# A build-time schedule with other durations for products and transfers (hybrid decoder, fp32 by split products)

## The chip, the cores and the metric

The kernel runs on one core of one Trainium2 chip. The time is the device time of one execution in microseconds; a version's time is the median of its runs. The engines are TensorE (PE, with its weight loads as PEld), VectorE (DVE), ScalarE (ACT), GpSimd (POOL) and the DMA queues (SP's, ACT's and POOL's among them). Each engine carries out its own instructions in the order in which they were emitted.

## The reference

Two layers of a decoder trunk, computed for a prompt of 2048 tokens and for 8 samples of one token each, all float32, width 1024. Cut to the parts that matter here:

```python
# layer 0: one projection feeds a convolution module and a gated delta rule
p = rms_norm(x, g) @ w_in
glu_val, glu_gate, gate_a, qkv, z, beta_l, a_l = split(p)
c = depthwise_conv31(glu_val * sigmoid(glu_gate))
a_out = silu(layer_norm(c + dw_b)) * silu(gate_a)
q, k, v = silu(depthwise_conv4(qkv))
b_out = rms_norm(gated_delta_rule(l2norm(q), l2norm(k), v, beta, g)) * silu(z)
x = x + concat(a_out, b_out) @ w_out
# layer 1: windows of 2, 4, 8, 16 tokens on four channel groups
u, gate = split(rms_norm(x, g) @ w_in_odd)
x = x + ((group_linear(window_mean(u) - u)) * scale * silu(gate)) @ w_out_odd
# behind each of the two: attention to a memory of 256 rows
x = x + softmax(rms_norm(x, g) @ wq @ mem_k.T / 16) @ mem_v @ wo
y = rms_norm(x, g)
```

The prompt and the samples share the weights. The samples have their own convolution states, delta-rule states and memory caches. The new states and the projected memory (keys and values) are outputs too.

## The kernel before

**Products.** A float32 operand is split into a high part (rounded to fp32r) and the rest. Each product is then three fp32r products: high by high, low by high, high by low. The splits of a weight tile `rraw` are the tiles `rhi` (a cast, on ScalarE or VectorE) and `rlo` (a subtraction, on VectorE or GpSimd); those of an activation are `hh`/`hl`, `h`, `xh`/`xl`, `mh`/`ml` by stage. `ps_mm` names the PSUM tile of all these products; there are three banks of it. The small float32 products of the side work go to the pool `bgp` (`ps_bg`, `ps_ss`, `ps_bc`, `ps_cs` and others).

**Stages.** There is one stream of 15,920 `ps_mm` products, the dense stream. It runs through the memory's keys and values (products of 256 columns), phase 1 (the input projection, `dense_main`, in pieces of 512, 512, 512, 512 and 260 tokens), the fill (`Fill.run`: memory keys times query weights and values times output weights, into DRAM tensors `d_G` and `d_VW` by way of `gv`), `e2` (layer 0's output projection, first product `xh,rhi`), the attention of layer 0, the odd mixer and the attention of layer 1.

**Side work.** Everything else hangs on that stream as generators:

- `conv31` runs 8 halves of the 31-tap convolution on VectorE, each of 30 steps `cacc<-glu,dww,cacc` of 1024 columns, 240 in all; `conv4` runs the 4-tap one (`qacc`).
- `fin_val` writes `glu`, which also frees a PSUM bank of the dense stream.
- `sample_mix` is the samples' mixer of layer 0; its first TensorE product is `ps_cs<-m_sq,ones`.
- `phase2` is the delta rule, in chunks, beside the fill.
- `sample_attn` is the samples' attention; it reads the caches into `a_big` and has row sums spread through DRAM tensors `d_sq` and `d_sp`.
- `square_sum`, `token_rstd` (`ps_ss`) and `spread` (`ps_bc`) are the norm's three steps: sum of squares, reciprocal root per token, and its spreading over the partitions.

**What sets the order.** The class `Flow` (L56 to L387) emits every instruction, and it keeps an assumed time for each engine in `t`. An instruction starts, by this account, when its engine is free and its operands are there, and takes a cost that is a formula in the number of columns. For VectorE and ScalarE these are, for instance, columns/0.96 + 130 ns for `scalar_tensor_tensor` with a scalar operand (L222) and columns/1.2 + 51 or more for an activation (L175). After each dense product, `pump` (L342) looks through the side tasks. It takes the next step of the first one whose own assumed time is not beyond that of TensorE, as long as neither ScalarE nor VectorE is ahead of TensorE by more than a limit (L62: 1500 or 3500 ns). So assumed costs alone fix where in the dense stream each side instruction stands, on every engine. They also choose engines: `move` and `rows` choose between ScalarE and VectorE, and `ve` between GpSimd and VectorE, by which would be done first by the assumed times. A store that has only ScalarE behind its data goes to ScalarE's DMA queue, any other to SP's (L294). A DMA's assumed landing decides when the tasks that read it may go on.

The costs that the change touches are in `mm` (L163) and `_dma` (L292); `spread` (L437) and `tok_spread` (L1486) are touched too.

Of the kernel before, what the change touches and what calls it, by code (L numbers as in the profile page):

```python
# [7 lines left out]
F32 = mybir.dt.float32  # L8
F32R = mybir.dt.float32r
# [14 lines left out]
def fsz(ap):  # L24
    n = 1
    for s in ap.shape[1:]:
        n *= s
    return n
# [27 lines left out]
class Flow:  # L56
# [106 lines left out]
    def mm(self, out, lhsT, rhs, start=True, stop=True, cost=None):  # L163
        n = fsz(rhs)
        if cost is None:
            cost = max(n, 248) * 0.422 if lhsT.dtype == F32R else max(n, 64) * 1.69
        self.pe_op(cost, out, lhsT, rhs)
        self.nc.tensor.matmul(out, lhsT, rhs, start=start, stop=stop)  # L168

# [122 lines left out]
    def _dma(self, out, in_, eng, t):  # L292
        ri, ro = [self.region(in_)], [self.region(out)]
        if eng == "sync" and out.space == DRAM and self.hand.get(in_.tensor.name) == {"act"}:  # L294
            eng = "scalar"
        s = max(self.t[eng], t, self.ready(ri, ro, eng))
        nb = 4
        for _, c in out.ap:
            nb *= c
        if eng == "scalar":  # L300
            s = max(s, self.t["act"])
            self.t["act"] = self.t[eng] = g = s + 360
        elif eng == "gpsimd":
            s = max(s, self.t["pool"])
            self.t["pool"] = self.t[eng] = g = s + 1060
        else:
            self.t[eng] = s + 50
            s = max(s, self.hw)
            self.hw = g = s + 475
        x = max(g + 650, self.ring)  # L310
        self.ring = x + nb / 360.0
        self.mark(ri, ro, "dma", self.ring, self.ring + 900)
        getattr(self.nc, eng).dma_start(out=out, in_=in_)

    def split(self, hi, lo, src, eng="dve", scale=1.0):
# [121 lines left out]
def spread(F, C, pool, ppool, r, n, tag, dg=None):  # L437

    ncn = (n + 127) // 128
    if dg is None:  # L440
        dg = pool.tile([128, ncn * 128], F32, tag=tag + "dg", name="dg")
    for c in range(ncn):
        F.ts(dg[:, c * 128:(c + 1) * 128], C.ident, r[:, c:c + 1], ALU.mult)
    yield
    ps = ppool.tile([128, 512], F32, tag="bg", name="ps_bc")
    F.mm(ps[:, 0:n], C.ones, dg[:, 0:n])
    return ps


def ceil128(n):  # L450
    return (n + 127) // 128 * 128
# [200 lines left out]
def phase1(F, C, I, D, st, P, R, mmp, bgp, loaders, mix, hp):  # L652
# [38 lines left out]
    with F.tile_pool(name="x1", bufs=1, side="right") as xp:  # L691
# [59 lines left out]
        def norms():  # L751
            for t, (o, n) in enumerate(DT):
                yield lambda: t in sums and (t < 4 or "kv" in sums)
                dg = xp.tile([128, 512], F32, tag="dg", name="dg", bufs=1)
                bc = yield from spread(F, C, xp, bgp, sums[t], n, "n", dg)
                for k in range(8):
                    x, _ = xs.pop((t, k))
                    F.stt(x, x, C.g_mix[:, 0, k:k + 1], bc[:, 0:n], ALU.mult, ALU.mult)
                    if k == 7:
                        F.now()  # L760
                    yield
                    F.copy(hs(t, 0, k), x)
                    yield
                    F.tt(hs(t, 1, k), x, hs(t, 0, k).bitcast(F32), ALU.subtract, eng=F.ve(n))
                    hfree.give()
                yield
                hdone.add(t)
# [716 lines left out]


def tok_spread(F, C, W, r, n):  # L1486
    return spread(F, C, W.p, W.bgp, r, n, "w", dg=W.t("sqq", [128, ceil128(n)]))


def mm3(F, R, W, name, j, x, n):  # L1490
# [12 lines left out]
def e2(F, C, W, I, D, st, R, bdone, over, grow, spawn):  # L1503
# [7 lines left out]
    def norm():  # L1511

        for g in range(NG):
            n = gn(g)
            yield lambda: g < 2 or g - 2 in used
            c = W.t("cd"[g % 2], [128, 4, n])
            load_cols(F, c, cv, g)
            yield
            cs = W.t("sqa", [128, n])
            F.red(cs, kt(c), ALU.add)  # L1520
            yield
            ps = W.bgp.tile([128, 512], F32, tag="bg", name="ps_mean")
            F.mm(ps[:, 0:n], C.ones, cs)
            F.stt(c, ps[:, 0:n].unsqueeze(1).to_broadcast([128, 4, n]), -1.0 / 512, c, ALU.mult, ALU.add)
            yield
            acc = square_sum(F, W, c, n)
            yield
            r = tok_rstd(F, C, W, acc, n, 1.0 / 512)
            yield
            ps = yield from tok_spread(F, C, W, r, n)  # L1530
            F.tt(c, c, ps[:, 0:n].unsqueeze(1).to_broadcast([128, 4, n]), ALU.mult)
            yield
            for q in range(4):
                F.act(c[:, q, :], c[:, q, :], AF.Silu, scale=C.lng[:, q:q + 1], bias=C.lnb[:, q:q + 1])
            ln[g] = c
# [71 lines left out]
def attn(F, C, W, D, st, R, l, xin, xout):  # L1607
# [130 lines left out]
    def final(g, y):  # L1738
        yield W.sq.ok
        W.sq.take()  # L1740
        acc = None
        for h in range(2):
            acc = square_sum(F, W, y[h], 256, acc, h == 1, "pool" if g < NG - 1 else "dve")
        yield
        r = tok_rstd(F, C, W, acc, 256, 1.0 / 1024)
        yield
        ps = yield from tok_spread(F, C, W, r, 256)
        W.sq.give()
        for j in range(8):
            h, q = j // 4, j % 4  # L1750
            F.stt(y[h][:, q, :], y[h][:, q, :], C.g_fin[:, j:j + 1], ps[:, 0:256], ALU.mult, ALU.mult)
            if q % 2:
                F.dma(D.o_y[g][:, j - 1:j + 1], y[h][:, q - 1:q + 1, :])
        if g + 2 < NG:
            ys[g + 1] = load_y(g + 1)
        ydone.add(g)
# [23 lines left out]
def odd_u(F, C, W, I, D, st, R, rr):  # L1780
# [5 lines left out]
    def prep():  # L1786
        for g in range(NG):
            n = gn(g)
            yield lambda: ("x", "o", g) in st.done and (g > 0 or "s0" in st.done)
            res = W.xbuf if g % 2 == 0 else W.mbuf  # L1790
            acc = None
            for h in range(2):
                x = W.t("f", [128, 4, n])
                F.dma(x, D.x2[g][:, 4 * h:4 * h + 4])
                yield
                acc = square_sum(F, W, x, n, acc, h == 1)
                if h == 0:
                    yield res.ok
                    res.take()
                    xs = W.pair("x" if g % 2 == 0 else "m", n)  # L1800
                yield from split_steps(F, xs[0][:, 4 * h:4 * h + 4], xs[1][:, 4 * h:4 * h + 4], x)
            ready[g] = xs, res
            yield
            r = tok_rstd(F, C, W, acc, n, 1.0 / 1024)
            F.vcopy(rr[:, g, 0:r.shape[1]], r)
            yield
            ps = yield from tok_spread(F, C, W, r, n)
            if g == 0:
                W.rb = W.t("rb", [128, 2, 264])
            rdone[g] = W.rb[:, g % 2, 0:n]  # L1810
            F.vcopy(rdone[g], ps[:, 0:n])
# [831 lines left out]
```

## Time and profile before

| | |
|---|---|
| median of 3 runs | 2902.09 us (2898.34 to 2905.38) |
| profiled execution | 2902.86 us, span 2901.1 us |
| mean granted TensorE clock in it | 0.972 |
| busy: TensorE, VectorE, ScalarE, GpSimd | 94%, 68%, 36%, 23% of the span |
| mean DMA rate | 130 GB/s |

By the dense stream's place, the trace has the memory products up to some 95 us, phase 1 from there to 826 us, the fill with the delta rule from 826 to 1164 us, and `e2` from 1200 us on. The odd mixer and the two attentions take the rest. The shares are means over stages that differ: VectorE's 68% is 94% in part of phase 1 and 54% at the end of it. A row of a group of instructions gives line, engine, operation, tile written and tiles read, shape and count, then the busy time and the mean duration in ns, then the idle time of the engine just ahead of them with what ended it. A row of the timeline gives start and duration in us, and in brackets the idle time before it. A float32 product leaves two records in the trace, an fp32r product one.

### The profile page before, as it was taken

To read this page: it belongs to the slowest core of one execution; us is meant where nothing else is said; L and a number is where in the kernel's file an instruction comes from. 1 tells how busy PE (TensorE), PEld (TensorE's weight loads), DVE (VectorE), ACT (ScalarE), POOL (GpSimd) and SP (SyncE) were. 2 spreads that over 40 slices of the span, in tenths; PEclk is the share of its full clock that TensorE was granted. 3 is DMA by queue.
4 is the path that set the end of the run, shared out by engine and by line. 5 is a ranking of instruction groups with operands and counts; after the bars stand their busy time and mean duration, and the time that the engine had idled before them with its cause. 6 is when DMAs were issued, how large, how long until landed. Compare 5 with 4: busy or idle time off the path is not lost.

```text
span 2901.1 us, 52440 instructions
## 1 busy us (share of the span) xinstructions
PE 2730.5 (94%) x20202; PEld 2498.5 (86%) x20202; DVE 1968.4 (68%) x4612; ACT 1032.0 (36%) x2448; POOL 657.0 (23%) x936
## 2 busy tenths in 40 slices
PE   7999999999998889799999999899999998999997
PEld 6878888888888778699898889899999997789987
DVE  6838999988667887776655556867755445765453
ACT  5632232233356455432321325443422122432321
POOL 3301112111054355122232320111011111221210
PEclk9999999999989899899999999999999999999998
DMA  7611122123455557565645434322545556422211
GB/s 240 213 48 41 46 75 65 46 77 113 129 148 160 154 165 230 172 228 183 211 149 169 144 117 140 116 70 74 173 134 165 181 165 206 136 78 68 70 59 52
DMA packets 269194, 377.85 MB, mean 130 GB/s; under 512 B 46096, under 2 KB 168208, under 8 KB 268944
## 3 DMA queue, kind: packets, MB, share of 16 engines
q1 hardware_dynamic: 211776, 264.77, 29.4%
q0 software_dynamic: 20864, 67.39, 7.5%
q10 hardware_dynamic: 36304, 42.34, 4.2%
q8 instruction: 159, 2.61, 0.4%
q14 instruction: 91, 0.75, 0.1%
HBM read 276.38 MB, written 96.40 MB: 128 GB/s over the span
## 4 chain that ended last, share of the span: by engine, by line
PE 34%; DMA 9%; DVE 6%; issue 2%; ACT 1%; POOL 1%; DVEq 0%; SPq 0%; POOLq 0%; ACTq 0%
PE ps_mm L168 32%; DMA a_big<-d_sp 2%; DVE a_big L225 1%; DMA a_big<-d_sq 1%; DMA a_big<-in_cache_v 1%; PE ps_pt L172 1%; DMA w_f<-d_x 1%; DVE rlo L225 1%; DVE w_d L219 1%; DMA rraw<-d_VW 1%; PE ps_row L168 1%; DVE rlo L219 1%; DVE ml L219 0%; DMA rraw<-d_G 0%; DMA a_big<-in_cache_k 0%
## 5 line engine op out<-in xcount | busy, mean ns | idle before, releaser
L219 POOL TENSOR_TENSOR rlo<-rraw,rhi 128x512 fp32r<-128x512 f32 x143 | 209.1, 1470 | 579.0 <-ACT rhi L186 495.5
L225 DVE SCALAR_TENSOR_TENSOR cacc<-glu,dww,cacc 128x1024 f32<-128x1024 f32 x240 | 325.6, 1369 | 5.9 <-ACT cacc L186 1.4
L219 POOL TENSOR_TENSOR w_sqb<-w_sqb,w_sqq 128x512 f32<-128x512 f32 (+1 forms) x101 | 137.1, 1357 | 660.9 <-ACT w_sqq L186 653.9
L168 PE MATMUL ps_mm<-xh,rhi 128*128 128x256 f32 (+1 forms) x1920 | 274.0, 285 | 5.3 <-DVE pool_sm L219 3.2
L168 PE MATMUL ps_mm<-xl,rhi 128*128 128x256 f32 (+1 forms) x1920 | 273.1, 284 | 0.0
L168 PE MATMUL ps_mm<-xh,rlo 128*128 128x256 f32 (+1 forms) x1920 | 272.7, 283 | 0.0
L168 PEld LDWEIGHTS ps_mm<-xh,rhi 128*128 128x128 f32 x1920 | 250.6, 192 | 8.6 <-issue 3.4
L168 PEld LDWEIGHTS ps_mm<-xl,rhi 128*128 128x128 f32 x1920 | 250.0, 192 | 2.6
L168 PEld LDWEIGHTS ps_mm<-xh,rlo 128*128 128x128 f32 x1920 | 248.2, 191 | 1.0
L168 PE MATMUL ps_mm<-hh,rhi 128*128 128x512 f32 (+2 forms) x1152 | 216.8, 329 | 20.2 <-ACT hh L186 15.8
L219 DVE TENSOR_TENSOR w_y<-ps_mm,w_y 128x256 f32<-128x256 f32 (+1 forms) x248 | 103.4, 420 | 165.6 <-PE ps_mm L168 161.2
L168 PE MATMUL ps_mm<-hh,rlo 128*128 128x512 f32 (+2 forms) x1152 | 214.6, 328 | 0.0
L168 PEld LDWEIGHTS ps_mm<-hh,rhi 128*128 128x128 f32 x1152 | 177.9, 191 | 42.0 <-ACT hh L186 16.2
L168 PE MATMUL ps_mm<-hl,rhi 128*128 128x512 f32 (+2 forms) x1152 | 211.7, 326 | 0.0
L225 DVE SCALAR_TENSOR_TENSOR a_big<-a_big 128x256 f32<-128x256 f32 x256 | 105.0, 448 | 144.5 <-DMA a_big<-d_sp 78.3
L186 ACT ACTIVATE rhi<-rraw 128x512 fp32r<-128x512 f32 x235 | 143.8, 628 | 164.0 <-DMA rraw<-d_G 41.5
L168 PEld LDWEIGHTS ps_mm<-hh,rlo 128*128 128x128 f32 x1152 | 175.9, 191 | 19.4 <-issue 2.2
L168 PEld LDWEIGHTS ps_mm<-hl,rhi 128*128 128x128 f32 x1152 | 175.4, 190 | 17.3
L168 PE MATMUL ps_mm<-mh,rhi 128*128 128x256 f32 (+1 forms) x1152 | 170.1, 288 | 11.8 <-ACT mh L186 11.7
L168 PE MATMUL ps_mm<-ml,rhi 128*128 128x256 f32 (+1 forms) x1152 | 170.5, 290 | 2.5 <-DVE ml L219 2.5
L168 PEld LDWEIGHTS ps_mm<-mh,rhi 128*128 128x128 f32 x1152 | 153.6, 195 | 14.5 <-ACT mh L186 12.8
L168 PE MATMUL ps_mm<-mh,rlo 128*128 128x256 f32 (+1 forms) x1152 | 165.6, 284 | 0.0
(425 smaller groups left out, 5344.5 us busy)
## 6 DMA issues: line engine op xcount, KB each, us to landing
w_f<-d_x SPq DMA_DIRECT2D x60, 512.0 KB
d_x<-w_y SPq DMA_DIRECT2D x44, 512.0 KB
w_y<-d_x SPq DMA_DIRECT2D x44, 512.0 KB
a_big<-in_cache_k POOLq DMA_DIRECT2D x64, 256.0 KB, 4.0
a_big<-in_cache_v POOLq DMA_DIRECT2D x64, 256.0 KB, 4.1
rraw<-in_w_in SPq DMA_DIRECT2D x56, 256.0 KB
d_qkv<-so ACTq DMA_DIRECT2D x48, 256.0 KB
rraw<-in_w_xk SPq DMA_DIRECT2D x32, 256.0 KB
```

Source lines behind the costliest of these rows:

```text
L168: self.nc.tensor.matmul(out, lhsT, rhs, start=start, stop=stop)
L172: self.nc.tensor.transpose(out, in_, ident)
L186: self.nc.scalar.activation(out=out, in_=in_, func=func, scale=scale, **kw)
L219: self._e(eng).tensor_tensor(out=out, in0=a, in1=b, op=op)
L225: self._e(eng).scalar_tensor_tensor(out=out, in0=a, scalar=s, in1=b, op0=op0, op1=op1, **kw)
```

## The change

It alters two assumed costs and the moment at which one pool is looked up.

```diff
@@ class Flow, mm
         if cost is None:
-            cost = max(n, 248) * 0.422 if lhsT.dtype == F32R else max(n, 64) * 1.69
+            cost = max(n, 240) * 0.426 + 9 if lhsT.dtype == F32R else max(n, 64) * 1.69
@@ class Flow, _dma
-        x = max(g + 650, self.ring)
-        self.ring = x + nb / 360.0
-        self.mark(ri, ro, "dma", self.ring, self.ring + 900)
+        x = max(g + 925, self.ring)
+        self.ring = x + nb / 270.0
+        self.mark(ri, ro, "dma", self.ring, self.ring + 1000)
@@ spread
     yield
-    ps = ppool.tile([128, 512], F32, tag="bg", name="ps_bc")
+    ps = getattr(ppool, "bgp", ppool).tile([128, 512], F32, tag="bg", name="ps_bc")
@@ tok_spread
-    return spread(F, C, W.p, W.bgp, r, n, "w", dg=W.t("sqq", [128, ceil128(n)]))
+    return spread(F, C, W.p, W, r, n, "w", dg=W.t("sqq", [128, ceil128(n)]))
```

An fp32r product of 512 columns is now assumed to take 227.1 ns instead of 216.1, one of 260 119.8 instead of 109.7, and one of 256 118.1 instead of 108.0. A transfer of 256 KB is assumed to start 925 instead of 650 ns behind its issue, to occupy the ring for 971 instead of 728 ns, and to be seen 1000 instead of 900 ns later. The costs of VectorE, ScalarE and GpSimd stay as they were. `spread` is a generator that stops at `yield`, and the pool of `ps_bc` is now asked for when it goes on, not when it is called.

The dense stream keeps its order, and each engine has the same kinds of work; the side instructions stand elsewhere in the stream. Some also change their engine: 25 casts `rhi` and 8 copies `gv` go from ScalarE to VectorE, 2 `rlo` from GpSimd to VectorE, and a few rows of the delta rule from VectorE to ScalarE.

The first place is on TensorE in phase 1, around the first product of the samples' mixer, `ps_cs<-m_sq,ones` (`h` and `hh`/`hl` are the split activations, `rhi`/`rlo` the split weights). Before:

```order
L168 MATMUL ps_mm<-h_223,rhi 128x512
L168 MATMUL ps_mm<-h_224,rhi 128x512
L168 MATMUL ps_mm<-h_225,rhi 128x512
L168 MATMUL ps_cs<-m_sq,ones 128x64
L168 MATMUL ps_mm<-h_210,rlo 128x512
L168 MATMUL ps_mm<-h_211,rlo 128x512
```

Now:

```order
L168 MATMUL ps_mm<-hh_244,rhi 128x512 x8
L168 MATMUL ps_mm<-hl_245,rhi 128x512 x8
L168 MATMUL ps_mm<-hh_244,rlo 128x512 x8
L168 MATMUL ps_mm<-hh_239,rhi 128x512 x8
L168 MATMUL ps_mm<-hl_240,rhi 128x512 x8
L168 MATMUL ps_mm<-hh_239,rlo 128x512 x8
L168 MATMUL ps_cs<-m_sq,ones 128x64
L168 MATMUL ps_mm<-hh_234,rhi 128x260 x8
L168 MATMUL ps_mm<-hl_235,rhi 128x260 x8
```

`ps_cs` stands 64 dense products earlier: 48 of 260 columns and 16 of 512 that were ahead of it are now behind it.

The second place is on VectorE, the rows ahead of `m_sq`, which `ps_cs` reads (the `m_` tiles are the mixer's). Before:

```order
L225 SCALAR_TENSOR_TENSOR cacc<-glu,dww,cacc 128x1024 x2
L232 TENSOR_SCALAR m_s<-m_s 128x96
L242 RECIPROCAL m_s<-m_s 128x96
L225 SCALAR_TENSOR_TENSOR cacc<-glu,dww,cacc 128x1024 x2
L219 TENSOR_TENSOR m_s<-m_s,m_x 128x96
L219 TENSOR_TENSOR m_sq<-m_s 128x64
L219 TENSOR_TENSOR rlo<-rraw,rhi 128x512
L225 SCALAR_TENSOR_TENSOR cacc<-glu,dww,cacc 128x1024 x2
L232 TENSOR_SCALAR m_sq<-ps_cs 128x64
```

Now:

```order
L225 SCALAR_TENSOR_TENSOR cacc<-glu,dww,cacc 128x1024 x2
L232 TENSOR_SCALAR m_s<-m_s 128x96
L242 RECIPROCAL m_s<-m_s 128x96
L225 SCALAR_TENSOR_TENSOR cacc<-glu,dww,cacc 128x1024 x2
L219 TENSOR_TENSOR m_s<-m_s,m_x 128x96
L219 TENSOR_TENSOR m_sq<-m_s 128x64
L232 TENSOR_SCALAR m_sq<-ps_cs 128x64
L415 TENSOR_SCALAR ri<-m_sq 128x64
```

Around it the rows are nearly the same, but ahead of `m_sq` there are now 238 of the 240 `cacc` steps instead of 224, and no work stands between `m_sq` and the reading of `ps_cs`.

The third place is on TensorE at the end of the fill (`rhi`, `rlo` with no `x` are the fill's operands; `x`, `vn`, `qk`, `o` are the delta rule's, `w_sqa` the next stage's norm). Before, the last rows of 95 side products in a row:

```order
L168 MATMUL ps_bg<-x,A 128x128 x4
L168 MATMUL ps_mean<-w_sqa,ones 128x256
L168 MATMUL ps_bg<-vn,kd 128x128 x4
L168 MATMUL ps_bg<-vn,qk 128x128 x4
L172 MATMUL ps_bg<-ident,o 128x128 x4
L168 MATMUL ps_ss<-ones,w_sqa 128x64 x2
L168 MATMUL ps_mm<-xh,rhi 128x264 x8
```

Now:

```order
L168 MATMUL ps_mm<-rhi 128x512 x2
L168 MATMUL ps_mm<-rlo,rhi 128x512 x2
L168 MATMUL ps_mm<-rhi,rlo 128x512 x2
L172 MATMUL ps_bg<-ident,o 128x128 x4
L168 MATMUL ps_mean<-w_sqa,ones 128x256
L168 MATMUL ps_ss<-ones,w_sqa 128x64 x2
L172 MATMUL ps_bg<-ident,o 128x128 x4
L168 MATMUL ps_mm<-xh,rhi 128x264 x4
```

Eleven side products are left between the fill's last product and the first of `e2`; the other 84 stand earlier, between products of the fill.

## The prediction

> **What bounds the kernel now.** I read the page's first part, then the busy time by stretches, then the waits inside those stretches, and last the single rows around the longest waits.
>
> ```profile
> span 2901.1 us, 52440 instructions
> PE 2730.5 (94%) x20202; PEld 2498.5 (86%) x20202; DVE 1968.4 (68%) x4612; ACT 1032.0 (36%) x2448; POOL 657.0 (23%) x936
> ```
>
> TensorE is busy 94% of the span, so the program is a stream of products, and the time moves only where that stream stands still, 2901.1 - 2730.5 = 170.6 us in all. The change reorders; the products are the same and in the same order among themselves. So the question is what happens to those 170.6 us, and 68% for VectorE is an average that hides a stage where it is full:
>
> ```profile
> core 0: us, PE busy (x) PEld busy (x) DVE busy (x) ACT busy (x) POOL busy (x), PEclk, DMA share, GB/s
> 243.00:566.00 323.00, 314.37 (x1689) 272.83 (x1688) 302.40 (x294) 88.92 (x168) 53.87 (x41) 0.99 0.19 59
> 566.00:702.00 136.00, 133.73 (x725) 116.13 (x723) 124.62 (x147) 48.69 (x88) 21.94 (x16) 1.00 0.29 90
> 750.00:800.00 50.00, 50.00 (x293) 42.83 (x292) 27.00 (x104) 21.30 (x78) 0.00 (x0) 1.00 0.41 121
> 826.00:1164.00 338.00, 297.72 (x3710) 267.36 (x3710) 262.71 (x807) 192.22 (x653) 163.99 (x313) 0.91 0.61 175
> 1164.00:1200.40 36.40, 23.35 (x175) 21.12 (x175) 29.62 (x74) 19.42 (x50) 5.55 (x6) 0.76 0.59 177
> ```
>
> From 243 to 702 us (the input projection with the 31-tap convolution on VectorE) VectorE works 302.40 of 323 and 124.62 of 136 us. What it waits for there is ScalarE, and what TensorE waits for is VectorE:
>
> ```profile
> DVE qacc L225 <- ACT qacc L186: 15.5, 18, 1.0
> ...
> DVE qacc L225 <- ACT qacc L186: 8.7, 10, 1.0
> ...
> PE ps_mm L168 <- DVE glu L225: 8.1, 4, 3.8
> ```
>
> The first two rows are the waits of 243 to 566 and of 566 to 702 us (total us, times, longest). They fill most of what VectorE has left: 302.4 + 15.5 of 323 and 124.6 + 8.7 of 136. So VectorE is one unbroken chain there, and already the pace setter: TensorE waits four times, 8.1 us, for a `glu` product on it to give a PSUM bank back. The chain ends here:
>
> ```profile
> 561.35 5.53 PE L168 MATMUL ps_mm<-h,rhi 128*128 128x512 f32 x16 [3.78 <-DVE glu L225]
> ...
> 690.07 1.12 PE L168 MATMUL ps_mm<-hh,rhi 128*128 128x260 f32 x8
> ...
> 695.84 3.83 PE L168 MATMUL ps_mm<-h,rhi 128*128 128x512 f32 x16
> 701.95 0.66 PE L168 MATMUL ps_cs<-m_sq,ones 128*128 128x64 f32 x2 [2.27 <-issue]
> ...
> 701.62 0.23 DVE L219 TENSOR_TENSOR m_sq<-m_s 128x64 f32<-128x64 f32 x1
> ```
>
> TensorE stops 2.27 us ahead of `ps_cs`, the first product of the sample's mixer. The row names no releaser, but `m_sq`, its operand, ends at 701.85 on VectorE, 0.1 us before it starts.
>
> **The change, part by part.**
>
> *Phase 1: the main term.* With dearer products and unchanged VectorE entries, the plan believes that VectorE gets more done under a stretch of TensorE, and issues its work earlier in the product stream. The entries of VectorE are below the trace: a `cacc` step stands at 1024/0.96 + 130 = 1197 ns.
>
> ```profile
> L225 DVE SCALAR_TENSOR_TENSOR cacc<-glu,dww,cacc 128x1024 f32<-128x1024 f32 x240 | 325.6, 1369 | 5.9 <-ACT cacc L186 1.4
> L219 DVE TENSOR_TENSOR rlo<-rraw,rhi 128x512 fp32r<-128x512 f32 x157 | 118.4, 769 | 36.2 <-ACT rhi L186 33.2 <-PE ps_mm L168 2.4
> L238 DVE CAST rhi<-rraw 128x512 fp32r<-128x512 f32 x65 | 34.9, 542 | 11.3 <-PE ps_mm L168 5.8 <-DMA rraw<-d_VW 2.2 <-DMA rraw<-in_w_xqT 1.8
> ```
>
> It takes 1369. Counted in the order of VectorE, `m_sq` now has 238 of the 240 `cacc` steps ahead of it instead of 224, 3 more `rlo`, and 1 more cast: 14 x 1.369 + 3 x 0.769 + 0.542 = 22.0 us. VectorE has nothing to skip there, so `m_sq` ends near 701.9 + 22.0 = 723.9. On TensorE `ps_cs` stands 64 products earlier than before (16 of 512 columns and 48 of 260), at the place that the old run passes at 690.07: the rows from there to 699.67 are those 64. So TensorE, if nothing else held it, would stand from 690.07 to 723.9: 33.8 us later than before at that place. From this the old stall goes, 2.27, since the 64 products now follow. Two things come on top: the short chain behind `ps_cs` loses cover (+2, the size of the stall that it replaces), and the clock is low after a long stop: at 561.35, after 3.78 us of waiting, 16 products took 5.53 instead of 3.83 us, so +1.7. Some of the 33.8 comes out earlier, as longer waits for `glu`: ahead of the second, third and fourth `glu` group VectorE has 6.3, 14.4 and 19.8 us more, by the same counts and rows. That is not added, as it is the same chain of VectorE. Sum: 33.8 - 2.3 + 2 + 1.7 = 35.2; I take +34, as the work that comes forward also begins up to 4 us before 243 us, where VectorE has room. Bounds: 24 (that, and a third of the 24.2 us of waits on ScalarE gone, since more work is queued) and 38 (neither, and the following chain doubles its loss). The time is not given back: what VectorE no longer has to do comes off 750 to 800 us, where it works 27 of 50 us and TensorE 50 of 50.
>
> By a rule of the Trainium skill (Perfetto Trace Analysis, section "Optimizing Scalar/DVE Operations") work goes off VectorE to ScalarE when VectorE is saturated; the change does the reverse with 25 weight casts. The rule bears on one of them by the order, which is in the 22.0 already; were all 25 on the path, the other 24 x 0.542 would be 13 us more.
>
> *End of the fill: a gain.* The fill's last product and the next stage's first stand 36 us apart:
>
> ```profile
> 1163.48 0.63 PE L168 MATMUL ps_mm<-rhi,rlo 128*128 128x512 f32 x2
> ...
> 1182.11 1.06 PE L168 MATMUL ps_bg<-vn,qk 128*128 128x128 f32 x8
> 1183.00 1.12 PE L168 MATMUL ps_bg<-S,k 128*128 128x128 f32 x8
> ...
> 1199.54 1.12 PE L168 MATMUL ps_ss<-ones,w_sqa 128*128 128x64 f32 x4 [4.96 <-POOL w_sqa L219]
> 1200.41 2.11 PE L168 MATMUL ps_mm<-xh,rhi 128*128 128x264 f32 x8
> ...
> 1188.26 1.93 DVE L246 TENSOR_REDUCE w_sqa<-w_d 128x256 f32<-128x1024 f32 x1
> ```
>
> Between them lie 95 side products of the delta rule, its output norms and the next stage's norm; TensorE is busy 23.35 us of the 36.4 at a clock of 0.76. In the changed order 11 of the 95 are left there and 84 stand up to 96 products earlier, inside the fill. What remains is the chain from the reduction at 1188.26 to `ps_ss` at 1199.54, 11.3 us, and about 2 us to the first product: gap 13, which is -23. The 84 products cost the fill what they take. Four of the commonest kind (two records each) take 0.89 us, from 1182.11 to 1183.00, or 0.22 each; two fifths of the 95 are that long and the others, of 64 columns or 64 rows, about half of it, so I take 0.14 for a mean, 13 us for the 95 and 11.6 for the 84. And the fill stage gets more of VectorE: 3 casts, 8 copies of fill results and 5 `b` copies that were ScalarE's,
>
> ```profile
> L232 DVE TENSOR_SCALAR gv<-ps_mm,g_x 128x256 f32<-128x256 f32 x23 | 10.6, 480 | 9.3 <-DMA d_G<-gv 7.0 <-ACT gv L186 2.0 <-DMA d_VW<-gv 0.3
> L238 DVE COPY gv<-ps_mm 128x512 f32<-128x512 f32 x13 | 8.8, 684 | 3.8 <-PE ps_bg L168 2.5 <-DMA d_G<-gv 1.2
> ```
>
> which is 3 x 0.542 + 4 x 0.480 + 4 x 0.684 and some 3 for the rest, about 9 us on an engine with 338 - 262.7 = 75 us of room; I let a third of it, +3, reach TensorE. Sum: -23 + 11.6 + 3 = -8. Bounds: -22, if the 84 products fit into waits that the fill has already (its TensorE is idle 338 - 297.7 = 40 us), and +10, if they come in lumps with no dense product between: the longest run of side products grows from 168 to 328.
>
> *The start.* The first norm's two products keep their chain, 8.6 us apart:
>
> ```profile
> 33.88 1.00 PE L168 MATMUL ps_ss<-ones,acc 128*128 128x64 f32 x8
> ...
> 42.44 1.65 PE L168 MATMUL ps_bc<-dg,ones 128*128 128x512 f32 x2 [3.25 <-DVE dg L232]
> ```
>
> In the new order 12 dense products cover it instead of 36, 24 fewer of 0.11 us: 2.6, and I take +2.5. Bounds 0 (the weight loads set the start) and 6.
>
> *The sample's attention* is moved later, by 50 to 150 products in the first layer and up to 356 in the second. Where it hurts now,
>
> ```profile
> PE ps_mm L168 <- ACT mh L186: 11.7, 4, 7.7
> PE ps_bc L168 <- DVE w_sqq L232: 11.4, 4, 3.4
> ...
> DVE a_big L225 <- DMA a_big<-d_sp: 38.2, 13, 5.1
> DVE a_big L225 <- DMA a_big<-d_sq: 36.7, 13, 5.2
> ```
>
> (2200 to 2500 us), VectorE stands in its queue for a small transfer, and the norm's operands behind it make TensorE wait 23 us. A later issue helps only if the wait begins later than the transfer. The distance from the issue to the first use stays at 25 to 30 products, or 3 us of 256 columns, against waits of up to 5.2. So 0; bounds -12 (half of the 23 goes) and +8 (the second layer's part meets the last stage).
>
> *The looked-up pool* at `spread` and `tok_spread` emits the same products into the same pool: 0, no operation has changed.
>
> *The sum*, against the profiled run, whose time is 2902.86 us (0.8 above the runs' median): 2902.9 + 34 - 8 + 2.5 + 0 = **2931 us**. A difference of 0.2%, 5.8 us, is what I call no change.
>
> **Rivals.**
>
> *1. VectorE's holes close, and it is faster.* The 24.2 us that VectorE waits for ScalarE ahead of `qacc` could be filled by the `cacc` steps that come forward. Then phase 1 costs 34 - 24 = 10, and with the fill at its best end: 2902.9 + 10 - 22 + 2.5 = 2893. It decides if those waits fall below 10 us in sum. For it: `cacc` needs nothing from ScalarE but its first value. Against: the copy and the three steps of `qacc` are issued in one go, so the first step is next in VectorE's queue whatever stands ahead. 0.10.
>
> *2. The fill hides its new products wholly.* Phase 1 at its low bound, fill at -22: 2902.9 + 24 - 22 + 2.5 = 2907, no change. For it: 40 us of idle TensorE in 826 to 1164. Against: these waits are for VectorE and ScalarE, which the same edit loads further. 0.14.
>
> *3. The fill loses too.* The lump of 328 side products and the copies put on VectorE cost more than the gap at the end gives: 2902.9 + 34 + 10 + 2.5 = 2949. For it: VectorE is 78% busy in the fill, and dense products wait for its `gv` copies. Against: the new order's shortfalls of cover, edge by edge, are about the old ones. All casts on the path would bring 2931 + 13 = 2944, the same end. 0.14.
>
> *4. It does not do what it says.* Then nothing would follow from "the durations of the traces". But it does, for what it names:
>
> ```profile
> 300.64 1.98 PE L168 MATMUL ps_mm<-hh,rlo 128*128 128x512 f32 x8
> 302.45 1.98 PE L168 MATMUL ps_mm<-hh,rhi 128*128 128x512 f32 x8
> ...
> 1263.99 1.10 PE L168 MATMUL ps_mm<-xl,rhi 128*128 128x256 f32 x8
> 1264.93 1.10 PE L168 MATMUL ps_mm<-xh,rlo 128*128 128x256 f32 x8
> ...
> a_big<-in_cache_k POOLq DMA_DIRECT2D x64, 256.0 KB, 4.0
> ```
>
> Eight products of 512 columns start 1.81 us after the eight before them, 226 ns each, and the new entry is 227.1 (old 216.1); at 256, 0.94 us, 117.5 ns, and the new entry is 118.1 (old 108.0). A load of 256 KB lands after 4.0 us, and the new entries give 1.06 + 0.93 + 0.97 + 1.0 = 3.96. The Trainium skill (TensorE: Matmul & The Clock Gate, section "Wait — 56ns, not 53.3ns?") has 215.7 ns from start to start at 512 columns, which would make the old entry the true one; the rows above disagree, and they decide. No chance of its own: the fault I see is that one side of the balance is corrected and VectorE's, 13% too low for its commonest step, is not.
>
> **How the numbers follow.** Forecast 0.62, its own range 2914 to 2946; rival 1 0.10, rival 2 0.14, rival 3 0.14. The range that holds 8 of 10 leaves out most of rival 1 and the top of rival 3: 2897 to 2952. Faster by over 0.2% means below 2896.3: rival 1 and a little of rival 2, 0.11. Within 0.2%, up to 2907.9: most of rival 2 and the low end of the forecast, 0.13. Slower: 0.76.
>
> **What would show it.** In the changed profile: TensorE standing still for some 35 to 45 us in sum (10.4 now) between 300 and 730 us, at `glu` rows and at `ps_cs`, with `m_sq` on VectorE near 724; VectorE busy to over 90% through it. Between the fill's last product and the first `xh` product 10 to 16 us instead of 36.9. Busy TensorE time unchanged but for some clock. The prediction is wrong in its main step if `m_sq` ends before 712, or if TensorE reaches the place of `ps_cs` later than `m_sq` does; it is wrong in the fill if the stage from 826 us to the first `xh` product takes longer than its 374 us of now.

## The result and the profile after

The changed kernel takes 2941.80 us in the median of 4 runs (2940.91 to 2947.33), against 2903.68 before (4 runs): a ratio of 1.0138, with a 95% interval of 1.012 to 1.0157. It is slower by 38 us, or 1.4%. The profiled execution took 2940.91 us, its span 2939.2. First the page's first part, after the change:

```profile
span 2939.2 us, 52470 instructions
PE 2741.8 (93%) x20202; PEld 2508.2 (85%) x20202; DVE 1991.0 (68%) x4651; ACT 1016.8 (35%) x2421; POOL 650.1 (22%) x936
```

The same products take TensorE 11.3 us longer (2741.8 against 2730.5), and it stands still for 26.8 us more (197.4 against 170.6). Both parts matter below: the mean granted clock is 0.964 against 0.972, and products right behind a stop take longer.

As the dense products have the same order in both kernels, the start of product k can be compared directly. The table gives, in us, its start in the profiled execution before, its delay in that of the change, and what each stage added of it.

| dense product | 1136 (start over) | 4200 (phase 1 over) | 4783 (fill's last) | 4784 (first `xh`) | 12000 | 14000 | 15919 (last) |
|---|---|---|---|---|---|---|---|
| before, start at us | 208.5 | 820.7 | 1163.7 | 1200.4 | 2256.6 | 2569.7 | 2883.9 |
| delay of the change | +11.5 | +36.6 | +76.0 | +66.2 | +54.4 | +34.4 | +38.1 |
| added by the stage | +11.5 | +25.1 | +39.4 | -9.8 | -11.8 | -20.0 | +3.7 |

The stages of phase 1, fill and gap in the view by stretches, first after, then before (the columns are those of the prediction's table):

```profile
220.00:857.00 637.00, 611.50 (x3311) 530.67 (x3310) 532.67 (x710) 184.71 (x394) 87.96 (x102) 0.97 0.23 72
857.00:1239.70 382.70, 323.49 (x3886) 291.88 (x3885) 289.12 (x886) 199.88 (x679) 167.24 (x323) 0.89 0.56 160
1239.70:1266.60 26.90, 4.95 (x16) 2.57 (x14) 18.13 (x44) 7.73 (x19) 2.00 (x2) 0.56 0.64 196
```

```profile
208.50:820.70 612.20, 601.29 (x3314) 522.38 (x3313) 529.14 (x701) 185.77 (x396) 95.93 (x103) 0.99 0.24 75
820.70:1163.70 343.00, 298.52 (x3719) 268.26 (x3718) 263.17 (x807) 191.92 (x653) 168.67 (x324) 0.91 0.61 174
1163.70:1200.40 36.70, 23.65 (x176) 21.12 (x175) 29.89 (x75) 19.72 (x50) 5.55 (x6) 0.76 0.59 178
```

Phase 1 is 25 us longer: 10.2 of them are busy time of the same products (611.5 against 601.3, clock 0.97 against 0.99), the other 15 are waits. The view of TensorE's waits in phase 1 (225 to 862 us) says which, and the timeline shows the place of `ps_cs`:

```profile
PE ps_mm L168 <- ACT raw L186: 8.9, 5, 3.4
PE ps_mm L168 <- DVE glu L225: 8.9, 4, 4.5
PE ps_cs L168 <- issue: 7.4, 1, 7.4
```

```profile
719.17 1.98 PE L168 MATMUL ps_mm<-hh,rlo 128*128 128x512 f32 x8
728.53 0.66 PE L168 MATMUL ps_cs<-m_sq,ones 128*128 128x64 f32 x2 [7.38 <-issue]
...
728.20 0.23 DVE L219 TENSOR_TENSOR m_sq<-m_s 128x64 f32<-128x64 f32 x1
```

Before, the three were 0.5, 8.1 and 2.3 us. `m_sq` ends at 728.4 on VectorE and `ps_cs` starts right behind it, 7.4 us after TensorE was ready. The `raw` row is nearly new. ScalarE's copy `raw<-ps_mm` gives a PSUM bank back to TensorE, and it stands on ScalarE behind a step `qacc<-raw,scw`, which waits for a small copy on VectorE, `raw<-raw`, that stands behind convolution steps. One of the five places, on ScalarE and then on VectorE:

```profile
655.71 0.72 ACT L186 ACTIVATE qacc<-raw,scw 128x512 f32<-128x512 f32 x1 [8.29 <-DVE raw L238]
656.34 0.61 ACT L186 ACTIVATE so<-qacc 128x512 f32<-128x512 f32 x1
656.86 0.57 ACT L186 ACTIVATE raw<-ps_mm 128x512 f32<-128x512 f32 x1
```

```profile
650.42 5.12 DVE L225 SCALAR_TENSOR_TENSOR cacc<-glu,dww,cacc 128x1024 f32<-128x1024 f32 x4
655.46 0.16 DVE L238 COPY raw<-raw 128x3 f32<-128x3 f32 x1
```

So ScalarE, and TensorE behind it, wait for VectorE there too.

At the end of the fill, the gap is now 26.9 us, with 11 side products in it (14 records). TensorE in it, and then ScalarE:

```profile
1239.30 1.05 PE L168 MATMUL ps_mm<-rhi,rlo 128*128 128x512 f32 x2
1240.48 0.63 PE L172 MATMUL ps_bg<-ident,o 128*128 128x128 f32 x4
1246.80 1.19 PE L168 MATMUL ps_mean<-w_sqa,ones 128*128 128x256 f32 x2 [5.70 <-DVE w_sqa L246]
1260.16 1.11 PE L168 MATMUL ps_ss<-ones,w_sqa 128*128 128x64 f32 x4 [12.17 <-POOL w_sqa L219]
...
1266.64 1.25 PE L168 MATMUL ps_mm<-xh,rhi 128*128 128x264 f32 x4 [3.49 <-DVE z L225]
```

```profile
1254.62 0.63 ACT L186 ACTIVATE rhi<-rraw 128x512 fp32r<-128x512 f32 x1 [7.87 <-DMA rraw<-in_w_out_e]
...
1256.75 0.61 ACT L186 ACTIVATE w_sqb<-w_d 128x512 f32<-128x512 f32 x1
1257.27 0.61 ACT L186 ACTIVATE w_sqq<-w_d 128x512 f32<-128x512 f32 x1
```

On ScalarE a weight cast `rhi` stands ahead of the norm's squares (`w_sqb`, `w_sqq`) and waits 7.87 us for its load. The squares, GpSimd's sum and `ps_ss` wait behind it.

Over fill and gap TensorE is idle for 81.2 us instead of 57.5: 14.7 us more in the fill and 9.0 more in the gap. The other 6 of the 29.6 us that are lost there are busy time.

### The profile page after: what moved, and what is told of

Its sections match the earlier page's. It is cut to its first block, busy times and chain, and to the rows that moved or that the text cites. A ratio compares the mean times of both kernels' runs of the same rounds, so it can differ in the third digit from the quotient of the medians.

```text
span 2939.2 us, 52470 instructions
## 1 busy us (share of the span) xinstructions
PE 2741.8 (93%) x20202; PEld 2508.2 (85%) x20202; DVE 1991.0 (68%) x4651; ACT 1016.8 (35%) x2421; POOL 650.1 (22%) x936
## 3 DMA queue, kind: packets, MB, share of 16 engines
q1 hardware_dynamic: 214160, 266.08, 29.1%
## 4 chain that ended last, share of the span: by engine, by line
PE 53%; DVE 24%; DMA 8%; issue 4%; ACT 3%; POOL 1%; SPq 1%; DVEq 0%; ACTq 0%; POOLq 0%
PE ps_mm L168 45%; DVE cacc L225 9%; PE ps_bg L168 3%; DVE qacc L225 3%; DMA a_big<-d_sq 1%; DMA a_big<-d_sp 1%; PE ps_row L168 1%; PE ps_pt L172 1%; DVE a_big L225 1%; DVE rlo L219 1%; DVE w_d L219 1%; DMA rraw<-d_G 1%; DVE rt L219 1%; PE ps_bg L172 1%; SPq L313 1%
## 5 line engine op out<-in xcount | busy, mean ns | idle before, releaser
L168 PE MATMUL ps_mm<-hh,rhi 128*128 128x512 f32 (+2 forms) x1152 | 220.4, 333 | 25.5 <-ACT hh L186 15.4
L186 ACT ACTIVATE rhi<-rraw 128x512 fp32r<-128x512 f32 x210 | 128.4, 628 | 151.4 <-DMA rraw<-d_G 38.9
```

Source lines behind the costliest of these rows:

```text
L186: self.nc.scalar.activation(out=out, in_=in_, func=func, scale=scale, **kw)
```

## The experiments

Stages are given by dense product as above: the start up to 1136, phase 1 to 4200, fill and gap to 4784 (379.7 us before, 409.3 in the change), the rest. Where a stage has old entries and another new ones, the class `Flow` was given a pair of switches that change at those places; all else is the changed kernel. With the old entries up to the fill's end (e4) TensorE has there the order of before. Each ratio is against runs of the old kernel beside it (medians 2897 to 2900 us), with its 95% interval; the stages are from the profiled execution, which can stand some us from the median.

**e1 and e2: one entry each.**

```diff
# e1: only mm's entry is new.  e2: only _dma's three are new.
-STAGE = ((1, 1), (1, 1), (1, 1), (1, 1))    # (product, transfers) for start, phase 1, fill, rest
+STAGE = ((1, 0), (1, 0), (1, 0), (1, 0))    # e1
+STAGE = ((0, 1), (0, 1), (0, 1), (0, 1))    # e2
```

> Only the product entry is changed; the three transfer entries are the old ones. Theory (VectorE is late because dearer products let the plan put more convolution steps ahead of the sample's mixer): m_sq has 236 cacc steps ahead of it (224 before, 238 in the change) and ps_cs stands at dense product 3668 (3744 before, 3680 in the change), so the delay at the end of phase 1, against before, is 20 to 30 us and the whole 2920 to 2950. Rival (the transfer entries carry the loss): phase 1 ends within 8 us of before, the whole near 2903.

> Only the three transfer entries are changed. Theory: the order of phase 1 is nearly the old one (224 cacc steps ahead of m_sq, ps_cs at product 3744), so phase 1 itself, from product 1136 to 4200, takes as long as before within 5 us; what is left is the start and the fill. Rival: phase 1 loses 15 us or more here too.

Measured: e1 3000.34 us, ratio 1.0352 (1.0327 to 1.0376); e2 2937.39 us, 1.0136 (1.0115 to 1.0157). In the trace of e1 phase 1 adds 26.6 us, in that of e2 it takes 0.9 less than before. So phase 1's loss comes from the product entry alone. The start loses by either (8.8 and 14.5). The rest shows what I had not looked for: between products 12000 and 14000, the samples' attention of layer 1, e2 gains 29.1 us and e1 1.5. The gain in that attention belongs to the transfer entries. The whole of e1 lies 50 us above the 2950 that I expected at most, as it loses 68 us behind the fill, 65 of them between 4784 and 12000. There TensorE waits 37.6 us for GpSimd's `w_sqa` at the norm's `ps_ss`, against 15.0 before, and its busy time grows by 20.8 us. Why that order puts `ps_ss` so badly was not followed. e2 loses 32 us in the same stretch, where one wait at `ps_ss` takes 23.8 us.

**e3: the new entries in phase 1 alone.**

```diff
+STAGE = ((0, 0), (1, 1), (0, 0), (0, 0))
```

> The new entries hold in phase 1 alone (from the end of the memory products to the start of the fill); before and behind it the old ones. Theory (the stages add up): 0 at product 1136, +25 us (20 to 32) at product 4200, then an order of the fill of its own; the whole 2915 to 2945. Rival (the loss of phase 1 is handed on from the start, which lost 11.5 us): under +10 at product 4200.

Measured: 2930.75 us, ratio 1.0119 (1.0092 to 1.0146). Phase 1 adds 25.0 us (delay 1.6 at 1136, 26.6 at 4200): the 25.1 of the change, with no loss handed on from the start. It is phase 1's own.

**e4: the new entries behind the fill alone.**

```diff
+STAGE = ((0, 0), (0, 0), (0, 0), (1, 1))
```

> The old entries up to the fill's end, the new ones from layer 0's output projection on. Theory (the changed kernel lost 66 us by the first xh product and won 28 back behind it, by its own order there): as before up to product 4784, then 28 us less (20 to 34), 2869 to 2883. Rival (what was won back was only work that the earlier stages had pushed ahead or that waited less because everything was late): 2898 to 2908.

Measured: 2890.80 us, ratio 0.9967 (0.9952 to 0.9983): faster by 0.33%, a third of what I expected. Up to the first `xh` product it is the old kernel (-0.6). Behind it 11.2 us are won: 18.4 between 12000 and 14000, less 7.2 lost ahead of it and behind it. So of the 28 us that the change won back behind the fill, the part in the samples' attention (20.0) is the new order's own. The other 8 are not in e4, which loses 3.8 between 4784 and 12000 where the change wins 11.8. Three more kernels with both new entries there and another end of the fill (e7, e9, e10) stand at -3.9, +1.6 and -0.1, so these 8 go with how the fill ended.

**e5: e3 with the sample's mixer held back.** The loss of phase 1 has two places, `ps_cs` and the waits for `glu` and `raw`. Here `ps_cs` may not stand ahead of product 3776. The mixer's later side products move with it, and nothing else on TensorE moves in phase 1 and the fill.

```diff
     F.tt(sq, s64, s64, ALU.mult)
-    yield
+    yield lambda: F.nd >= 3776          # F.nd counts the dense products
     ps = colsum(F, C, bgp, sq, 64)
```

> As e3_phase1_only, but the sample mixer's ps_cs may not stand ahead of dense product 3776 (it stood at 3680; 3744 before); every other row of TensorE in phase 1 and the fill stays. Theory A, the prediction's (the late m_sq at ps_cs is where the loss becomes final): the 10.7 us that e3 lost between products 3600 and 3700 go, and the delay at 4200 falls from 26.6 to some 5 to 12, since the waits for glu would be caught up. Theory B (the convolution steps that come early make VectorE late for glu and for raw long before, and TensorE never gets that back): 15 to 20 us stay at product 4200, the 19 of product 3600.

Measured: 2914.30 us, ratio 1.0056 (1.0037 to 1.0075). Phase 1 adds 14.6 us instead of 25.0. The waits of e3 and then of e5 in 208 to 850 us:

```profile
PE ps_mm L172 <- DVE glu L229: 10.4, 4, 4.5
PE ps_mm L172 <- ACT raw L190: 8.6, 5, 3.1
PE ps_cs L172 <- issue: 8.5, 1, 8.5
```

```profile
PE ps_mm L174 <- DVE glu L231: 10.3, 4, 4.5
PE ps_mm L174 <- ACT raw L192: 8.6, 5, 3.1
```

The 8.5 us at `ps_cs` are gone, and the other two rows are the same. The delay at product 4200 is 14.4 us, just under the 15 to 20 of theory B and above the 5 to 12 of theory A. So it is nearly theory B: the mixer's place is 10.4 of the 25 us, and the early convolution steps cost 17.7 by product 3600, of which TensorE gets 3.1 back by 4200.

**e6 and e7: VectorE's entry set to the trace as well.** In e6 in phase 1 alone, in e7 in the changed kernel.

```diff
     def stt(self, out, a, s, b, op0, op1, accum=None, eng="dve", dep=0):
-        c = 68 if isinstance(s, float) else 130
+        c = (68 if isinstance(s, float) else 130) + (158 if fsz(out) == 1024 and self.ph1 else 0)
```

> As e3_phase1_only, and the assumed cost of a cacc step in phase 1 is 1355 ns (its measured mean distance to the next start) instead of 1197. The ratio of cacc step to product of 512 columns is then 1355/227 = 5.97; it was 1197/216 = 5.54 before, 5.27 in the change, and 1355/226.5 = 5.98 in the trace. Theory (two errors cancelled, and the change mends one): m_sq has 222 cacc steps ahead of it and ps_cs stands at 3776, so the delay at product 4200 is between -10 and +4 instead of +26.6. Rival (the products' entry costs phase 1 something by itself, whatever VectorE's): +15 or more.

> The changed kernel with the cacc step at 1355 ns, everywhere else as changed. Theory: the start keeps its 11.5 us, phase 1 then adds nothing (product 4200 at +5 to +15 instead of +36.6). The fill gets another order, which I can't foretell: -9 to +30 by the five orders so far. The whole 2895 to 2930.

Measured: in e6 phase 1 takes 6.9 us less than before, in e7 3.7 less; in e3 and in the change it was 25 more. The whole is 2925.23 us in e6 (1.0084, 1.0059 to 1.011), as its fill and gap came out 9.5 us and its rest 19.2 us longer than before. It is 2894.57 in e7 (0.9989, 0.9973 to 1.0005), just under the range that I gave and not to be told from before. One number, the cost of the convolution step, takes back the change's loss of phase 1. The stretch of phase 1 in e6, and the waits in it (208 to 850 us), whose first row is the mixer again:

```profile
211.60:816.90 605.30, 597.03 (x3289) 518.58 (x3289) 524.62 (x673) 181.64 (x376) 82.06 (x74) 1.00 0.23 75
```

```profile
PE ps_cs L173 <- DVE m_sq L224: 4.1, 1, 4.1
...
PE ps_mm L173 <- DVE glu L230: 0.9, 2, 0.6
```

VectorE is as busy as before, the granted clock is 1.00, and of the 8.1 us that even the old kernel waited for `glu` 0.9 are left.

**e9: one nanosecond in the fill.**

```diff
# the first number is now the constant added to max(n, 240) * 0.426, 9 in the change
+STAGE = ((9, 1), (9, 1), (10, 1), (9, 1))
```

> The changed kernel, and in the fill alone the product entry is max(n, 240) x 0.426 + 10 ns instead of + 9. Nothing of the start and of phase 1 moves; in the fill the run of 328 side products at product 4424 is gone (the longest is now 184) and 42 side products instead of 11 stand in the gap at its end. Theory (the fill's 29.6 us are those of one order that a tiny shift makes, not of the entry's value): the stretch from product 4200 to 4784 changes by 8 us or more against the 409.3 us of the changed kernel; by the seven orders so far it lies between 368 and 409. Rival (the dearer products or the casts on VectorE, 87 here and 90 there, cost it): 402 to 416.

Measured: 2925.78 us, ratio 1.0093 (1.0072 to 1.0114), 16 us less than the change. Fill and gap take 382.0 us instead of 409.3:

```profile
854.50:1200.50 346.00, 299.18 (x3818) 271.56 (x3817) 269.69 (x829) 195.21 (x667) 165.71 (x322) 0.92 0.60 175
1200.50:1236.50 36.00, 14.02 (x78) 11.73 (x77) 22.88 (x66) 18.67 (x48) 0.00 (x0) 0.64 0.51 154
```

That is near the 379.7 of before. So the 29.6 us that the change lost there are no effect of dearer products or of casts on VectorE (87 in this kernel, 90 in the change). They belong to one order of the delta rule's steps between the fill's products, which a shift of 1 ns replaces by another. This run also takes away the run of 328 side products at product 4424, so by itself it does not clear that lump. The traces do: from product 4200 to 4536, with the lump inside, the change takes 231.7 us and TensorE is idle for 33.7, against 229.3 and 32.4 before, for nearly the same side work (2108 records against 2088). Its extra idle time comes behind that.

**e10: the cast put behind the squares**, in the changed kernel's gap.

```diff
-            if not self.can(b) or F.t["pe"] < t:
-                yield lambda: self.can(b) and F.t["pe"] >= t
+            if not self.can(b) or F.t["pe"] < t + F.gapx:
+                yield lambda: self.can(b) and F.t["pe"] >= t + F.gapx
...
         F.run(fill.run())
+        F.gapx, F.t1 = 4000.0, F.t["pe"] + 15000.0     # back to 0 beyond t1
```

> The changed kernel, and in the gap at the end of the fill the weight cast rhi that stood ahead of the norm's squares w_sqb and w_sqq on ScalarE now stands behind them; TensorE's order up to there is the same. Theory (that cast waited 7.87 us for its load, and the squares, GpSimd's sums and ps_ss waited behind it): the wait of ps_ss for w_sqa falls from 12.2 to some 4 to 6 us and the gap from 26.9 to 18 to 22 us; the whole some 5 us less than the change, if the first xh product finds its weights. Rival (the first xh product would have waited for those weights anyway): the gap stays at 25 to 28.

Measured: 2944.67 us, ratio 1.0153 (1.0126 to 1.0179), so nothing won. The gap did shrink, from 26.9 to 21.5 us, and the wait at `ps_ss` from 12.17 to 3.19, but other waits took part of the place:

```profile
1249.06 0.63 ACT L191 ACTIVATE w_sqb<-w_d 128x512 f32<-128x512 f32 x1 [0.61 <-DVE w_d L230]
...
1254.91 1.25 ACT L191 ACTIVATE rhi<-rraw 128x512 fp32r<-128x512 f32 x2 [4.70 <-DMA rraw<-in_w_out_e]
```

```profile
1255.68 1.12 PE L177 MATMUL ps_bg<-ident,o 128*128 128x128 f32 x4 [7.92 <-DVE o L224]
1259.99 1.08 PE L173 MATMUL ps_ss<-ones,w_sqa 128*128 128x64 f32 x4 [3.19 <-DVE z L230]
1260.84 1.23 PE L173 MATMUL ps_mm<-xh,rhi 128*128 128x264 f32 x4
1266.87 1.22 PE L173 MATMUL ps_bc<-w_sqq,ones 128*128 128x256 f32 x2 [4.81 <-DVE w_sqq L237]
```

The squares run 7.7 us sooner, but now the delta rule's last rows (`o`, `z`) hold TensorE for 7.92 and 3.19 us, and `ps_bc` waits 4.81 behind the first `xh` products. The cast was one of several chains that end within some 8 us of each other. Between 4784 and 12000 this run then takes 11.7 us longer than the change. Its fill, with the change's order on TensorE, takes 387.2 us against 382.4: a stage's time in one trace can be off by that much.

**e8, e11 and e12: versions put together from the better parts.** All have the old entries in the start, e6's phase 1 and the new entries behind the fill; e11 and e12 also hold `ps_cs` until product 3824, and e11 has another product entry in the fill.

```diff
+STAGE = ((0, 0), (1, 1), (0, 0), (1, 1))     # e8
+STAGE = ((0, 0), (9, 1), (10, 0), (9, 1))    # e11: numbers as in e9, 10 in the fill
+STAGE = ((0, 0), (9, 1), (0, 0), (9, 1))     # e12
```

> Old entries in the start and the fill, the new ones with a cacc step of 1355 ns in phase 1, the new ones behind the fill (e4's part). If the stages add up: phase 1 as in e6, the rest 11.2 us better as in e4; by that 2875 to 2895 unless the fill's new order costs. Rival (the part behind the fill depends on how the fill ended): the rest within 5 us of before.

> As e8_best_guess, with the mixer's ps_cs held until product 3824 (e6 and e8 waited 4.1 us there), and in the fill a product entry of max(n, 240) x 0.426 + 10 with the old transfer entries. Phase 1: delay -10 to -5 at product 4200. The fill's order is a new one: 368 to 409 us from 4200 to 4784 (380 before). The rest 11 us less. Sum: 2865 to 2920, middle 2885.

> As e11, with the old entries in the fill (its order still differs from before, as the fill begins in another state of the plan). Phase 1 and the rest as in e11, the fill 368 to 409 us: 2865 to 2920, middle 2885. Theory for both: the better one is as good as its fill's order, and the two differ there by more than 5 us.

Measured: e8 2897.85 us, 1.0003 (0.999 to 1.0017); e11 2895.79, 0.9986 (0.9971 to 1.0); e12 2894.44, 0.9986 (0.9971 to 1.0001). By their traces phase 1 is 3.9, 7.4 and 8.0 us better than before. Fill and gap take 387.8, 377.9 and 405.9 us, and the rest is 11.1, 0.2 and 31.7 us better. e8 lies 3 us above what I expected, as its fill cost 8.1. For e11 and e12 the theory was that the better fill makes the better kernel, and that failed: their fills differ by 28 us and their times by 1.4. e12 lost 26 us in the fill and got 32 back behind it. Only e4 stands clear of before, by 0.33%, and it beats both kernels.

## Why the prediction was right, and where it was not

The forecast was 2931 us, or 28 us more than before, and the measured time is 38 more. The direction and the mechanism of phase 1 were right. That the sum came within its range is luck: the fill was wrong by 37.6 us and what lies behind it by 28.1 the other way, the start by 9.0 and phase 1 by 8.9 the other way. Rival 3, in which the fill loses too, had 2949 and is 7 us off where the forecast is 11. Its loss in the fill came true, but not by the lump that it named (e9). Rival 1 did not happen: VectorE's waits ahead of `qacc` are 21.9 us instead of 24.1, far above its limit of 10. Term by term, forecast and measured (delays of the table above):

- **The start: +2.5, measured +11.5.** The step that failed is the count of the cover between `ps_ss` and `ps_bc` alone. The wait at `ps_bc` rises only from 3.25 to 3.99, but `ps_ss` itself comes 3.8 us later than before (at 33.88), behind a wait of its own, and the second pair loses as well, 4.01 us at its `ps_bc` against 1.21. The waits make up half of the loss, and the busy time of the same products the other half (188.2 us against 182.5). The first pair now:

```profile
37.72 1.10 PE L168 MATMUL ps_ss<-ones,acc 128*128 128x64 f32 x8 [1.89 <-DVE acc L219]
...
45.39 2.07 PE L168 MATMUL ps_bc<-dg,ones 128*128 128x512 f32 x2 [3.99 <-DVE dg L232]
```

Three other kernels with the same order of the start (e7, e9, e10) lost 6.0, 8.6 and 6.2 there, so 11.5 is at the top of what this order does.
- **Phase 1: +34, measured +25.1.** The mechanism stood, and e3 and e6 show it: dearer products against an unchanged VectorE put the convolution too early, VectorE falls behind, and TensorE waits for `glu`, for `raw` and at `ps_cs`. The size failed at the 22.0 us of VectorE ahead of `m_sq`. From 243 us on, where VectorE was full, they were 16.8. First before, then after, up to `m_sq`:

```profile
243.00:557.00 314.00, 309.15 (x1673) 268.78 (x1672) 293.51 (x288) 88.92 (x168) 50.95 (x39) 1.00 0.19 59
557.00:702.00 145.00, 138.94 (x742) 120.19 (x741) 133.52 (x153) 48.69 (x88) 24.86 (x19) 0.99 0.29 88
```

```profile
254.50:585.00 330.50, 317.61 (x1672) 275.94 (x1671) 310.40 (x305) 89.21 (x167) 46.78 (x37) 0.97 0.18 56
585.00:728.50 143.50, 131.21 (x678) 112.42 (x677) 133.45 (x151) 46.91 (x84) 24.83 (x18) 0.96 0.27 86
```

The extra convolution steps did take what was counted for them (13 of the 14 lie in this stretch, 18.4 us), but the `qacc` steps, as many as before, took 4.9 us less. Only 1.0 us more came ahead of the stretch, where the "up to 4 us" stood. `m_sq` ended at 728.4; without the start's delay that is 716.9, and not 723.9. "TensorE, if nothing else held it" was no good picture either: 14.6 of the 25 are waits for `glu` and `raw` and their clock, and stay when the mixer is held back (e5). The sign that I gave, 35 to 45 us of TensorE standing still between 300 and 730 us, failed too: it was 25.2, against 10.9 before.
- **The clock.** I had 1.7 us for one cold restart. The busy time of phase 1 grew by 10.2 us, with ten stops instead of six. Behind the longest, at `ps_cs`, the first two rows of eight products took 2.08 and 1.52 us, and 1.12 from then on. That the other stops account for the rest in this way was not added up.
- **The fill: -8, measured +29.6.** The step that failed is the gap of 13 us at its end and, more, the idea that the order of a fill can be costed by its counts. The gap was 26.9. I had taken the reduction as the gap's begin, 11.3 us from it to `ps_ss`, and 2 behind that. In the change it starts 5.1 us behind the start of the fill's last product:

```profile
1244.76 1.90 DVE L246 TENSOR_REDUCE w_sqa<-w_d 128x256 f32<-128x1024 f32 x1
```

From it to `ps_ss` are 15.4 us, as I had not followed the queue of ScalarE, where a cast that waits for a weight load stood ahead of the squares. From there to the first `xh` product are 6.5, as the delta rule's last `ident,o` products and `z` stand between. The fill itself took 39.4 us more instead of 14.6. e9 shows how much hangs on the order: with 1 ns more in the entry, fill and gap take 27.3 us less. Over the change and the twelve experiments they lie between 367.8 and 409.3 us, and before's order, at 379.7, was a good one among them. My bounds of -22 to +10 were far too narrow for a draw from that.
- **The samples' attention: 0, measured -20.0.** I said that VectorE's waits for the small transfers would remain, and they do. In 2254 to 2604 us, up to product 14000, they are

```profile
DVE a_big L225 <- DMA a_big<-d_sq: 42.9, 14, 5.3
DVE a_big L225 <- DMA a_big<-d_sp: 30.1, 10, 4.9
```

against 36.7 and 38.2 before (2200 to 2569 us). But TensorE waits less behind them for the norm's operands:

```profile
PE ps_mm L168 <- ACT mh L186: 5.2, 4, 3.0
PE ps_bc L168 <- DVE w_sqq L232: 5.1, 4, 2.0
```

They were 11.7 and 11.4, so the two rows account for 12.8 of the 20 us. Eight kernels with both new entries behind the fill, the change among them, gain 15 to 22 us between 12000 and 14000, e2 with the transfers alone 29, and the four with the old transfer entries there 0.3 to 3.7. I had the later place and the unchanged distance from issue to use, and did not ask which products wait behind the instruction that waits.

The fault that I named, one side of the balance corrected and VectorE's left low, is shown for phase 1 by e6 and e7. In the plan a convolution step was worth 1197/216 = 5.5 products of 512 columns, the change made it 5.3, and by the trace, with the 1355 ns that e6 and e7 assume, it is 1355/226.5 = 6.0. The old product entry was wrong in the direction that made up for part of VectorE's.

## What to carry to other kernels

A planner's costs act as ratios between engines. Setting one engine's to the trace can move the ratio away from it, as in phase 1. So set all engines of a saturated stage together, from distances between starts, and check the ratio. An order that falls out of such a plan in a stage with many short chains is one draw of many: a shift of 1 ns moved this kernel by 16 us. Judge such a change stage by stage, by the start of the same product in both traces. A stage's gain need not last when stages are put together: e4 kept one and won 0.33%, e8, e11 and e12 kept several and came out as before.

## What the runs showed of the hardware that was not expected

The `cacc` step of 1024 columns has three prices on VectorE. Of the 240 in the trace of before, those followed by another kind of instruction are 1.20 us from the next start, most of those followed by another `cacc` step 1.32, and 22 take 2.0 to 2.4 us. Each of these 22 overlaps a subtraction `rlo` on GpSimd; of the 217 of the usual length 20 do. Two stretches of the old trace, four steps each, without and with GpSimd beside them:

```profile
412.42 5.12 DVE L225 SCALAR_TENSOR_TENSOR cacc<-glu,dww,cacc 128x1024 f32<-128x1024 f32 x4
```

```profile
443.93 4.09 POOL L219 TENSOR_TENSOR rlo<-rraw,rhi 128x512 fp32r<-128x512 f32 x2 [36.00 <-ACT rhi L186]
...
444.88 6.74 DVE L225 SCALAR_TENSOR_TENSOR cacc<-glu,dww,cacc 128x1024 f32<-128x1024 f32 x4
```

The four steps take 6.74 instead of 5.12 us. The Trainium skill (SBUF — State Buffer, section "SBUF: two separate sides") says that VectorE, in an operation with two SBUF inputs, and GpSimd, in one that reads SBUF, take turns on one shared port pair, and that the one that starts first has it for its whole instruction. The trace agrees: all 22 slow steps end 1.08 us after the end of a subtraction that held them up, and in the 20 of usual length the subtraction begins after the step, or ends within 0.06 us of its start. One step of 1.49 us, in neither group, ends 1.08 us behind a subtraction as well. A slow step takes about 0.95 us more, which for the 22 is some 20 us of the engine that sets the pace in phase 1. A version that keeps `rlo` off GpSimd there was not tried.
